# A list schedule replaced by written tables of the order, the engines and the buffer places

## The chip, the cores and the metric

The kernel runs on one core of a Trainium2 chip. The metric is device time in microseconds. The page of the profile calls the engines PE (TensorE, the matrix engine), PEld (its weight loads, which overlap), DVE (VectorE), ACT (ScalarE), POOL (GpSimd) and SP (SyncE). SP and POOL issue the DMA transfers here; each engine runs its instructions in the order in which the program issued them, and waits at each for what it needs.

## The reference

One layer of a hybrid backbone runs on 1024 latent tokens and 128 context tokens, all in float32. Cut to what matters:

```
h = rmsnorm(x, w) * (1 + scale1) + shift1          # scales, shifts, gates from silu(c) @ ada_w
u = h @ w_in                                       # 1024 -> 4288 columns
o_a = hgrn2_mixer(u[..., :P_A])                    # 4 heads x 128, forward and backward
o_b = rwkv7_mixer(u[..., P_A:])                    # 8 heads x 64, delta rule, both directions
x = x + gate1 * (concat([o_a, o_b]) @ w_out)
h = rmsnorm(x, w) * (1 + scale2) + shift2
gt = conv(h @ ffn_w_gate) + b                      # 3x3 on the latent grid, width 3 on the context
x = x + gate2 * ((gelu(gt) * (h @ ffn_w_up)) @ ffn_w_down)
y = rmsnorm(x, final_norm_w)
```

The outputs are both y and the final context states of the two mixers.

## The kernel before

The work is done in stages, but their instructions are mixed with one another. Line numbers are those of the profile of before.

- Start: nine row blocks of x are loaded (L1214), normed (L1148 to L1151, L1216), transposed on PE (L1208) and modulated into `hh` and `hl`, a high and a low part in the float32r format. `mod_columns` makes the modulation from `ada_w` (L1246, L1252).
- Projections: `proj` multiplies columns of `w_in` with the tokens, three float32r products for each (L1139 to L1141: high by high, low by high, high by low), 8 steps deep and 384 tokens wide. `load_w` fetches a column of weights on SP (seen as L1345 and L1306) and splits it.
- `features` prepares RWKV (small products L1474, L1475; copies of keys and values to DRAM at L1436, L1497 to L1503), `elim` solves its small systems, `chains` walks 18 chunks in each of two groups (L1790, L1804, L1837, L1844, L1852, L1861, L1863), `hgrn_block` and `hgrn_out` do HGRN (L1630 to L1753), `ada_block` the rest of the modulation (L1039, L1046, L1054). `wo_tile` is the output projection (L2033 to L2035, transposes at L2047).
- FFN: `product` (L2145) multiplies gate and up weights with quarter matrices, seven products in place of eight; `ffn_mid` does the convolution on DVE (L2234). `three` (L2310) is the down projection. The last row block is finished in two halves of 256 columns (L2432 to L2451), whose accumulators share one PSUM bank.

What decides the order: the kernel's text does not issue its instructions directly. Each call is recorded by `Plan` as an `Op`: one instruction, or a group that stays together. `close` finds what an op must wait for from the addresses that it reads and writes. An op may have several forms: `st` may issue a store on POOL or SP, `copy` may run on ACT or DVE. A tile belongs to a `Tag`, which has one or more places in a buffer.

`Plan.schedule` then runs a list scheduler over all 9618 ops. It estimates a cost for each op (`cost`, `pe_cost`, `wire`), takes the engine that is free first, ranks the ready ops by the length of the work behind them plus a lead (`LEADS`, and `NUDGE`, a number for every 16 ops of a kind), and takes off something for a change of the array's shape (`INTO`, `OUT`, `SWITCH`) or of an activation table. It chooses the form with the engine and the place that comes free first. `plan.ahead`, `plan.follow` and `plan.mark` give it hints. `Plan.issue` issues the ops in that order, engine by engine, and the framework adds the semaphores.

Of the kernel before, what the change touches and what calls it, by code (L numbers as in the profile page):

```python
# [20 lines left out]
P = 128  # L21
# [11 lines left out]
STRETCH = 2.76  # L33
LEAD_LAST = -10.47
LEAD_ADA = -9.0
LATE = 1.2
SWITCH = 2.0
FULL = 128, 128
INTO = 2.76
OUT = 0.86  # L40
HAM = 3.413
QUIET = 0.65
FETCH = 42.0
AHEAD = 240.0
HUNGRY = 2.04
BUSY = 168.59
ADDS = 2.1
NUDGE = {'step_kernel': [-1, 21, 23, 153, 19, -118, 24, 0, 59, 53, 38, -46, 7, -86, -57, -200, -162, -34, -65, 27, -37], 'const': [-1], 'turned': [45, 73, 123, 24, -81], 'param_loads': [-52, -27], 'params': [30, 141], 'first_columns': [-17, 0, 65, 95], 'mod_columns': [-200, 49, -70, -62], 'modulated': [34, -122, 14, -97, -13], 'conv_rkv': [-20, 28, 17, 14, -71, 21, 7, 6, 7, -131, -59, 65, -34, 2, -24, -4, -58, -28, -9, -11, -21, 2, -23, -64, -4, -36, -50, 143, 184], 'features': [6, -9, -1, 3, -13, 173, 166, 184, 184, 200, 149, -20, -36, 7, -27, -39, -22, -14, -14, -15, -12, -8, -18, -9, -17, 82, -12, 36, 109, 0, -7, 18, 92, -2, -53, -32, -50, 170, 95, 183, 157, 182, 192, 192, 196, 200, 169, 125, 124], 'hgrn_in': [-38, 41, -10, -9, -4, -40, -6, 65, 16, 167, 157, 136, 29, 21, 50, 30, -3, 3, 39, 5, 70, 11, 10, -19, -11, -16, -2, 19, -8, -14, -25, -37, -36, -37, -25, -62, -36, 154, -52, -90, -82, -96, -30, -38, -41, -30], 'elim': [17, 87, 0, -32, 20, -28, -25, -4, 80, -14, 86, 4, -1, -24, -14, 125, 199, 146, 179, 149, 76, 38, 74, 27, -3, -39, 69, 52, 13, -2, -7, 191, 129], 'chains': [-12, 7, 58, 70, 29, 57, 1, -9, -1, -10, 16, 18, 0, 0, 0, 4, 77, -53, 16, 8, 3, 30, -18, 35, 32, -33, 115, -29, 18, 40, 129, 1, -4, -10, 90, 82, 83, 76, 73, 184, 142, 17, 51, 4, 4, -8, -27, -45, 7], 'prep': [49, -75, 0, 82, 43, 31, 99, -43, 1, 33, -8, -70, 33, 4, -101, -13], 'bonus_rows': [49, -35, -103, -31, -186, -64], 'ada_block': [22, 5, -21, 0, 29, 23, 26, -1], 'hgrn_block': [31, -19, 139, -23, -94, -50, -93, -134, -96, 62, 82, 78, -23, 4, 4, -19, -18, -26, 49, 152, 4, 8, -95, -27, -41, -25, 87, 42, -65, 27, -3, 1, 1, -7, -23, 13, 61, 142, 176, 187, -16, 16, 9, 84, 186, 25, 34, 45, 8, 90, 104, 54, 12], 'hgrn_out': [8, -12, -31, -29, -73, -7, 20, 37, 0, 0, -66, 42, -18, 184, 5], 'mod_scale': [-188], 'wo_tile': [132, -14, -52, -13, -77, -45, 20, 14, 138, 89, 184, 105, 112, 117, 153, -46, 13, 104, 153, 65, -75, -18], 'post': [-28, -39, 124, -84, 61, 182, 99, 91, 98], 'stored': [164], 'put': [140, 90, 106, -49, -44], 'made': [131, -57], 'weights': [43, -44, 92, 147, 0, 8, -8, -18, 5, -12, -25], 'pair': [136, -34, 76, -16, 38, 4, 105, 37, -22, 7, -52, 10, 19, 14, -44, -32, -22, 5, -84, -73], 'product': [57, 177, 42, 46, 40, 20, 5, -5, 140, 121, 38, 192, -114, 25, 53, 97, 54, 40, 49, 185, 179, 184, 178, 64, 29, 32, 149, -6, 103, -18, -10, 4, -3, -2, 7, 12, -12, -55, -74, -88, 2, 2, -67, 65, 177, 23, 4, 22, 27, 36, 30, 41, 29, 17, 18, -12, 3, -18, -25, -52, -68, -48, -48, -31, 55, 41, 21, -34, -36, -36, -40, -56, -12, -27, -91, 8, -65], 'save': [105, 108, 53, 55, 13, 120, 47, 53, -164], 'front': [-17, -5, -19, 21, 73, 183, -1, -45, -50, 40, -69, 12, -29, -153], 'ffn_mid': [17, 31, -149, -11, 18, -24, 58, 51, 21, -13, 12, -149, -127, -154, -22, 26, -32, -74, -118, -29, -29, -24, -71, -200], 'down_sums': [-199, -96, 3, 17, -130, -141], 'rows_of_context': [-128, -42], 'tokens': [-35, -200, -165, -57, 82], 'part': [0, -36, -65, 9, 57, 17, -87, -74, -146, -145, -30, -154, -32, -28, -32, -63, -90, -146, 34, 112, -141, 13], 'weight': [0, 144, 90, 47], 'three': [-92, -24, -50, 1, 34, -59, -24, -5, -112, -198, -194, -193, -26, -159, -162, 89, -9, 200, 91, 195, -48, -47, -45], 'gate_row': [-16], 'kept': [-48], 'gated': [-101, -117, 49, 200, 19], 'normed': [-200, 181, -22], 'put_out': [-155, -71], 'total': [-200, -13, -29]}
LEADS = {'ada_block': 46.4, 'bonus_rows': 27.8, 'chains': -35.7, 'const': 113.0, 'conv_rkv': 0.0, 'down_weights': -36.2, 'elim': -4.6, 'features': 0.0, 'ffn_down': 14.5, 'ffn_mid': -1.7, 'finish': 52.5, 'finish_last': -12.3, 'first_columns': -38.6, 'front': 0.0, 'gate_row': 0.0, 'hgrn_block': -3.6, 'hgrn_in': 0.0, 'hgrn_out': 113.5, 'late': -0.7, 'made': 3.5, 'mod_columns': -1.2, 'mod_scale': 70.4, 'modulated': -24.2, 'pair': 8.2, 'param_loads': 9.6, 'params': -96.8, 'post': 3.0, 'prep': 119.5, 'product': -3.4, 'put': 0.0, 'save': 4.8, 'step_kernel': -1.0, 'stored': 0.0, 'three': -10.1, 'total': -0.3, 'turned': 4.0, 'weights': 0.0, 'wo_tile': 5.1}
# [88 lines left out]

class Op:
    __slots__ = ("id", "forms", "reads", "writes", "deps", "succ", "tiles", "tail", "start", "end", "left", "est",  # L140
                 "cost", "mode", "after", "kind", "wait", "place", "table", "dense", "lead", "area", "port", "wire", "dma", "words")
# [36 lines left out]
class Plan:  # L178


    PIECES = ("proj", "small_proj", "norm_rows", "modulate", "gate_rows", "load_step", "load_values", "conv_tiles")
    HELPERS = ("mm", "st", "copy", "combine", "split", "load_w", "record", "either", "acc", "fetch")
    ENGINES = ("PE", "DVE", "ACT", "POOL", "SP")
    BITS = 23
    ROW = 1 << 16
    LOW = (1 << 23) - 1
    TABLES = {"Ln": 1, "Sqrt": 2, "Gelu_apprx_tanh": 3, "Exp": 0, "Tanh": 0}
    last = None

    def __init__(self, tc, base):  # L190
        nc = tc.nc
        self.base = {F32: base, F32R: base.bitcast(F32R), I32: base.bitcast(I32)}
        self.tc = tc
        self.units = {"PE": nc.tensor, "DVE": nc.vector, "ACT": nc.scalar, "POOL": nc.gpsimd, "SP": nc.sync}
        self.ops, self.tags, self.tiles = [], {}, [None]
        self.live, self.group, self.chain_end, self.lead, self.boxes = {}, None, {}, 0.0, []
        self.first, self.mark, self.seen = None, 0, {}
        Plan.last = self
# [42 lines left out]
    def add(self, forms):  # L241
# [4 lines left out]
        line = f.f_lineno  # L246
        while f.f_code.co_name in self.PIECES:
            f = f.f_back
        self.kind = f.f_code.co_name
        forms = [(e, [(m, a, k, line)]) for e, m, a, k in forms]  # L250
        if self.group is not None:
            self.group.append(forms[0])
# [2230 lines left out]
```

## Time and profile before

| | |
|---|---|
| median of 3 runs | 1796.35 us (1785.7 to 1799.57) |
| profiled execution | 1795.13 us, its span 1793.4 us |
| PE busy | 1727.2 us, 96% of the span |
| DVE, ACT, POOL busy | 1459.4, 932.5 and 444.0 us |
| mean granted clock of PE | 0.992 |
| DMA | 352.99 MB moved, mean 197 GB/s |

The span is the time between the first and the last instruction that the profile shows. A matmul's duration in it overlaps with that of the next, so the distance between two starts tells what one costs. An idle time is shown in square brackets with what ended it; "issue" means that nothing in the profile did.

### The profile page before, as it was taken

The page shows a single profiled execution, that of the slowest core. Times are in us where ns is not written, and L with a number is a line of the kernel's source. Part 1 is how long each engine was busy: PE and PEld are TensorE (multiplying, and loading weights), DVE is VectorE, ACT ScalarE, POOL GpSimd, SP SyncE. Part 2 cuts the span into 40 slices and gives each one's busy share as a digit, 9 for nine tenths or more (in the row PEclk, how much of TensorE's full clock was granted, in tenths as well). Part 3 has the DMA queues.
Part 4 walks back from the last instruction along what each step waited for, and adds up shares of the span by engine and source line. Part 5 has one row for each costly group of instructions (what it writes and reads, how often), then busy time and mean ns, then how long its engine had stood idle before and what let it go on. Part 6 is the DMA issues. An engine that isn't in the chain of part 4 may idle for free. (4 is left out here: it accounts for less than half of the span.)

```text
span 1793.4 us, 44872 instructions
## 1 busy us (share of the span) xinstructions
PE 1727.2 (96%) x17726; PEld 1548.7 (86%) x17726; DVE 1459.4 (81%) x2799; ACT 932.5 (52%) x1907; POOL 444.0 (25%) x708
## 2 busy tenths in 40 slices
PE   6999999999999989999999999999999999999998
PEld 4898888889988878887777889999999999888886
DVE  6559988987788868887777877998988889979875
ACT  6556757552266545663545754444444444665542
POOL 2003334263323222233211122233233333100000
PEclk9999999999999999999999999999999999999999
DMA  9326447497676578898987657678787778997674
GB/s 321 100 63 175 109 123 172 109 228 202 187 220 196 178 222 265 265 308 249 312 240 250 226 129 147 133 172 174 153 165 162 156 139 173 288 327 221 212 254 146
DMA packets 320148, 352.99 MB, mean 197 GB/s; under 512 B 66420, under 2 KB 238242, under 8 KB 319585
## 3 DMA queue, kind: packets, MB, share of 16 engines
q1 hardware_dynamic: 253520, 245.18, 45.7%
q0 software_dynamic: 66416, 104.95, 25.2%
q8 instruction: 139, 2.28, 0.5%
q14 instruction: 73, 0.59, 0.1%
HBM read 254.99 MB, written 118.10 MB: 208 GB/s over the span
## 5 line engine op out<-in xcount | busy, mean ns | idle before, releaser
L1139 PE MATMUL banks<-hh,wh 128*128 128x384 f32 x768 | 279.7, 364 | 1.4 <-DVE fx L1327 1.4
L1141 PE MATMUL banks<-hh,wl 128*128 128x384 f32 x768 | 258.4, 336 | 0.0
L1140 PE MATMUL banks<-hl,wh 128*128 128x384 f32 x768 | 258.1, 336 | 0.0
L2234 DVE SCALAR_TENSOR_TENSOR low<-low,pf 128x1024 f32<-128x1024 f32 x176 | 225.2, 1281 | 12.2 <-ACT low L2228 9.7
L2145 PE MATMUL banks<-qm,wh 128*128 128x320 f32 x968 | 223.5, 310 | 1.6 <-DVE low L2204 1.3
L2145 PE MATMUL banks<-hbm,wh 128*128 128x256 f32 x880 | 165.0, 284 | 1.5 <-DVE low L2013 1.5
L2145 PE MATMUL banks<-qm,wl 128*128 128x320 f32 x528 | 163.1, 309 | 0.2 <-DVE wl L2115 0.2
L2145 PEld LDWEIGHTS banks<-qm,wh 128*128 128x128 f32 x968 | 160.8, 189 | 2.1 <-DVE low L2204 1.5
L1139 PEld LDWEIGHTS banks<-hh,wh 128*128 128x128 f32 x768 | 144.9, 189 | 19.6 <-issue 10.9
L1140 PEld LDWEIGHTS banks<-hl,wh 128*128 128x128 f32 x768 | 145.2, 189 | 2.0 <-issue 1.2
L1141 PEld LDWEIGHTS banks<-hh,wl 128*128 128x128 f32 x768 | 144.6, 188 | 0.0
L2145 PEld LDWEIGHTS banks<-hbm,wh 128*128 128x128 f32 x880 | 140.3, 191 | 2.3 <-DVE low L2013 1.8
L2145 PE MATMUL banks<-ham,wh 128*128 128x256 f32 (+1 forms) x616 | 132.7, 295 | 0.0
L2145 PE MATMUL banks<-hbm,wl 128*128 128x256 f32 x440 | 124.8, 284 | 0.0
L2183 ACT COPY fx<-banks 128x320 f32<-128x320 f32 (+1 forms) x132 | 52.4, 398 | 111.6 <-PE banks L2145 111.6
L2145 PEld LDWEIGHTS banks<-ham,wh 128*128 128x128 f32 x616 | 102.1, 191 | 0.1
L2145 PEld LDWEIGHTS banks<-qm,wl 128*128 128x128 f32 x528 | 99.1, 188 | 0.8 <-DVE wl L2115 0.8
L2115 ACT CAST wh<-low 128x512 fp32r<-128x512 f32 x88 | 54.4, 619 | 65.8 <-DMA low<-in_ffn_w_up_dram 42.5
L2145 PEld LDWEIGHTS banks<-hbm,wl 128*128 128x128 f32 x440 | 84.4, 192 | 0.0
L2145 PE MATMUL banks<-ham,wl 128*128 128x256 f32 (+1 forms) x264 | 77.3, 293 | 0.0
L2115 DVE TENSOR_TENSOR wl<-low,wh 128x512 fp32r<-128x512 f32 x88 | 60.3, 687 | 9.9 <-ACT wh L2115 9.5
L2115 ACT CAST wh<-wr 128x512 fp32r<-128x512 f32 x66 | 39.8, 621 | 47.8 <-PE banks L2145 27.6
(595 smaller groups left out, 4444.1 us busy)
## 6 DMA issues: line engine op xcount, KB each, us to landing
wr<-in_w_in_dram SPq DMA_DIRECT2D x34, 512.0 KB, 5.5
d_t<-in_ffn_w_down_dram POOLq DMA_DIRECT2D x55, 256.0 KB, 6.3
low<-d_a SPq DMA_DIRECT2D x51, 256.0 KB, 5.3
low<-d_ak SPq DMA_DIRECT2D x64, 192.0 KB, 5.7
low<-in_ffn_w_gate_dram SPq DMA_DIRECT2D x44, 256.0 KB, 3.2
low<-in_ffn_w_up_dram POOLq DMA_DIRECT2D x44, 256.0 KB, 5.0
d_a<-low POOLq DMA_DIRECT2D x19, 576.0 KB, 4.0
low<-d_kb SPq DMA_DIRECT2D x36, 256.0 KB, 5.8
```

Source lines behind the costliest of these rows:

```text
L1139: mm(o, wh[:, kt, :], hh[:, kt, c], kt == 0, False)
L1140: mm(o, wh[:, kt, :], hl[:, kt, c], False, False)
L1141: mm(o, wl[:, kt, :], hh[:, kt, c], False, kt == KT - 1)
L2115: split(*w, src)
L2145: pe.matmul(o, a[:, kt, :], b[:, kt, :], start=start and first, stop=last, skip_group_check=not start)
L2183: act.copy(keep[n], y[:, 0:w])
L2234: dve.scalar_tensor_tensor(av, shifted(dy, dx), tap(3 * dy + dx), av, MUL, ADD)
```

## The change

`schedule` no longer plans. Three tables take the place of its decisions: `SEQUENCE`, the numbers of all ops in the order in which they are issued; `ENGINE_OF`, a letter for each of the 1500 ops that have more than one form; `PLACE_OF`, a digit for each tile whose tag has more than one place. They were found by a local search on the sequence itself. The costs, leads, nudges and hints go. The recorded work and the finding of dependences stay, and the assertions make sure that the order keeps the dependences and that no two live tiles share a place.

```
-STRETCH = 2.76
-LEAD_LAST = -10.47
...
-NUDGE = {...}
-LEADS = {...}
+SEQUENCE = [int(i) for i in """
+1 2 17 6 18 19 0 12 13 14 15 7 11 177 184 10 27 28 4 3 20 21 29 30 33 22 24 16 34 26 31 32
...
+""".split()]
+ENGINE_OF = (
+    "VVVAVAVAAAAAAVAVVVAVAAAVGGGGGSGGGGGSSGSSGGGAVAVVVAAVVVVAVVAVAAAAVVAVVVAAVVVVVAVAGASASASASASVSASVVAGAASVAVASGSSAAAASSGSAAASAASAAAASSSSVAVASGSSAA
...
+PLACE_OF = (
...
     def schedule(self):
-        ops = self.ops
-        for op in ops:
-            for d in op.deps:
-                ops[d].succ.append(op.id)
...
+        by = iter(ENGINE_OF)
+        for op in self.ops:
+            if len(op.forms) > 1:
+                e = self.LETTER[next(by)]
+                op.forms = [f for f in op.forms if f[0] == e]
+        spot = iter(PLACE_OF)
+        for rec in self.tiles[1:]:
+            t = rec[0]
+            rec[2] = t.places[int(next(spot), 36) if len(t.places) > 1 else 0]
+        self.order = [self.ops[i] for i in SEQUENCE]
...
-    with plan.ahead(900.0):
-        ld(cr[0], I["c"].rearrange("l (a b) -> (l a) b", b=128))
...
+    ld(cr[0], I["c"].rearrange("l (a b) -> (l a) b", b=128))
...
-                plan.follow("dense")
```

Compared op by op, half of the 9618 ops stand within 24 places of where they stood and one in a hundred over 162 away. Of the 1500 with a choice, 242 go from POOL to SP and 71 from SP to POOL, 138 from DVE to ACT and 61 from ACT to DVE, 23 from ACT to POOL and 14 back. Of the 2526 tiles with a choice 1547 lie elsewhere. SP issues 1185 DMAs (1014 before), POOL 357 (528), DVE has 2724 instructions (2801) and ACT 1942 (1872).

The changed file is shorter, so its lines have other numbers: L1139 to L1141 are now L1070 to L1072, L1659 is L1582, L1748 is L1671, L1804 is L1727, L1844 is L1767, L1852 is L1775, L2310 is L2229; L1345, L1306, L1436, L1497, L1500 and L1502 are L1268, L1229, L1359, L1420, L1423 and L1425.

The first place is on PE, in the mixed stage, where `chains` and `hgrn_block` run beside the fourth `ada_block`. `hh`, `hl`, `wh` and `wl` are a projection (full array), `low` to `low` with 64x64 a step of a chain (shape 128*64), `top` with 32x32 a step of HGRN (128*32), and `c_ident` a transpose (full array). Before:

```order
L1852 MATMUL banks<-low 64x64 x8
L1139 MATMUL banks<-hh,wh_133 128x384
L1140 MATMUL banks<-hl,wh_133 128x384
L1141 MATMUL banks<-hh,wl_135 128x384
L1804 MATMUL banks<-c_ident,low 128x128 x4
L1659 MATMUL banks<-top 32x32 x12
L1748 MATMUL banks<-c_ident,top 128x128 x3
L1844 MATMUL banks<-low 64x64 x8
L1659 MATMUL banks<-top 32x32 x12
L1139 MATMUL banks<-hh,wh_133 128x384
L1140 MATMUL banks<-hl,wh_133 128x384
L1141 MATMUL banks<-hh,wl_135 128x384
```

The same instructions in the change:

```order
L1775 MATMUL banks<-low 64x64 x8
L1582 MATMUL banks<-top 32x32 x12
L1727 MATMUL banks<-c_ident,low 128x128 x4
L1070 MATMUL banks<-hh,wh_134 128x384
L1071 MATMUL banks<-hl,wh_134 128x384
L1072 MATMUL banks<-hh,wl_135 128x384
L1671 MATMUL banks<-c_ident,top 128x128 x3
L1070 MATMUL banks<-hh,wh_134 128x384
L1071 MATMUL banks<-hl,wh_134 128x384
L1072 MATMUL banks<-hh,wl_135 128x384
L1767 MATMUL banks<-low 64x64 x8
L1582 MATMUL banks<-top 32x32 x12
```

The four groups on the full array stand together now, so the array's shape changes four times along these rows instead of six. Over the whole of PE's order it changes 445 times instead of 543.

The second place is the end of PE's order, the two halves of the last row block (`qm`, `ham`, `hbm`, `wh`, `wl` hold weights and activations there; three rows of one kind are one step). Semaphore waits are shown in brackets. Before:

```order
L2310 MATMUL banks<-qm,hbm 128x256 x3
L2310 MATMUL banks<-ham 128x256 [waits DVE_49]
L2310 MATMUL banks<-ham 128x256 x2
L2310 MATMUL banks<-qm,ham 128x256 [waits DVE_49]
L2310 MATMUL banks<-qm,ham 128x256 x2
L2310 MATMUL banks<-qm,hbm 128x256 x3
L2310 MATMUL banks<-qm 128x256 [waits Activation_49]
L2310 MATMUL banks<-qm 128x256 x2
L2310 MATMUL banks<-ham,qm 128x256 x3
```

In the change:

```order
L2229 MATMUL banks<-hbm,ham 128x256 x3
L2229 MATMUL banks<-ham,qm 128x256 [waits DVE_49]
L2229 MATMUL banks<-ham,qm 128x256 x2
L2229 MATMUL banks<-qm,wl_136 128x256 x3
L2229 MATMUL banks<-hbm,qm 128x256 x3
L2229 MATMUL banks<-qm,hbm 128x256 x3
L2229 MATMUL banks<-ham,hbm 128x256 x3
L2229 MATMUL banks<-wh_134,qm 128x256 x3
L2229 MATMUL banks<-qm,hbm 128x256 [waits Activation_49]
L2229 MATMUL banks<-qm,hbm 128x256 x2
```

One wait for DVE is gone, and six steps run between the two waits that are left; two more steps of the second half now stand behind the first half.

The third place is SP, early in `features`, between the fetch of a weight column for HGRN (`wr`, L1306) and the next one for RWKV (L1345); `d_kb`, `d_ak` and `d_v` are DRAM buffers that are stored to. Before:

```order
L1306 DMA wr<-in_w_in_dram 128x8x128
L1502 DMA d_kb_82<-top 64x6x64
L1500 DMA d_kb_82<-top 64x6x128
L1502 DMA d_kb_82<-top 64x6x64
L1500 DMA d_kb_82<-top 64x6x128
L1497 DMA d_ak_78<-top 128x6x128
L1345 DMA wr<-in_w_in_dram 128x8x128
```

In the change:

```order
L1229 DMA wr<-in_w_in_dram 128x8x128
L1425 DMA d_kb_82<-top 64x6x64
L1420 DMA d_ak_78<-top 128x6x128
L1423 DMA d_kb_82<-top 64x6x128
L1425 DMA d_kb_82<-top 64x6x64
L1359 DMA d_v_84<-top 128x3x128 x2
L1420 DMA d_ak_78<-top 128x6x128
L1425 DMA d_kb_82<-top 64x6x64 x2
L1268 DMA wr<-in_w_in_dram 128x8x128
```

Nine stores stand between the two fetches where there were five.

524 lines of the change are left out of this document (84 added, 440 removed), and 300 rows, old and new, of the table SEQUENCE.

## The prediction

> **What bounds the kernel now.** I read the page first, then the busy times by stage, then who PE waits for, then single stretches of the timeline.
>
> ```profile
> span 1793.4 us, 44872 instructions
> PE 1727.2 (96%) x17726; PEld 1548.7 (86%) x17726; DVE 1459.4 (81%) x2799; ACT 932.5 (52%) x1907; POOL 444.0 (25%) x708
> ```
>
> TensorE (PE) is busy for 96% of the span, so everything below is about PE: what time it idles, and what time it is "busy" without being useful. The next answer cuts the span into the start, the mixed stage (projections, RWKV and HGRN work), the dense stage (both halves of the FFN) and the tail. The first number after the window is its length, the next PE's busy time, then weight loads, VectorE, ScalarE and GpSimd; the last three are the granted clock, the DMA share and GB/s.
>
> ```profile
> core 0: us, PE busy (x) PEld busy (x) DVE busy (x) ACT busy (x) POOL busy (x), PEclk, DMA share, GB/s
> 0.00:36.00 36.00, 20.84 (x159) 14.48 (x159) 22.36 (x61) 23.94 (x50) 11.74 (x34) 1.00 0.96 315
> 36.00:1056.00 1020.00, 979.07 (x12869) 852.85 (x12867) 823.26 (x1813) 562.23 (x1202) 279.11 (x510) 0.99 0.68 200
> 1056.00:1781.00 725.00, 723.67 (x4687) 678.62 (x4686) 609.85 (x916) 344.25 (x650) 153.16 (x164) 1.00 0.76 189
> 1781.00:1793.40 12.40, 3.63 (x19) 2.72 (x17) 3.96 (x11) 2.03 (x6) 0.00 (x0) 0.65 0.20 75
> ```
>
> Idle time of PE is length less busy: 15.2 us in the start, 40.9 in the mixed stage, 1.3 in the dense stage, 8.8 in the tail. The dense stage cannot get faster by a new order: it has the same matmuls and nothing to fill. The start has its DMA engines 96% busy with bytes that the change does not alter. So the mixed stage is where an order can matter. PE's waits, longest in total first (us in total, times, longest):
>
> ```profile
> PE banks L1208 <- DVE top L1216: 6.3, 2, 5.2
> PE banks L1852 <- issue: 5.2, 2, 4.0
> PE banks L1208 <- DVE low L1149: 5.1, 1, 5.1
> PE banks L1474 <- DVE top L1465: 3.9, 3, 3.1
> PE banks L1790 <- DMA low<-d_ak: 3.0, 5, 1.3
> PE banks L1474 <- DVE top L1466: 2.4, 2, 1.2
> ...
> PE banks L1659 <- DVE top L1688: 1.1, 1, 1.1
> ```
>
> The two L1208 rows belong to the start. The others are many short waits, most of them for VectorE, at different lines. Only one is long: 4.0 us put down to nothing ("issue"), so no order of the work is shown to be its cause.
>
> **The change part by part.** No instruction is added or removed: 9618 records before and after, the same matmuls, the same transfers. What moves is the order, the engine of 1500 records that may go to either of two, and the place of tiles in their buffers. Half of the records stand within 24 places of where they stood, so this is a reshuffle nearby and not another plan.
>
> *Array shapes.* Every small matmul uses a part of the array, and the third column of the trace's rows says which (128*32, 128*64, 64*128 and so on). Here is what a change of shape costs, in the rows of one stretch (start, duration, then the line):
>
> ```profile
> 540.64 0.40 PE L1665 MATMUL banks<-top 128*32 128x32 f32 x24
> 540.97 0.44 PE L1139 MATMUL banks<-hh,wh 128*128 128x384 f32 x1
> 541.25 0.34 PE L1140 MATMUL banks<-hl,wh 128*128 128x384 f32 x1
> 541.42 0.34 PE L1141 MATMUL banks<-hh,wl 128*128 128x384 f32 x1
> 541.60 0.34 PE L1139 MATMUL banks<-hh,wh 128*128 128x384 f32 x1
> ...
> 542.47 0.34 PE L1141 MATMUL banks<-hh,wl 128*128 128x384 f32 x1
> 542.73 0.57 PE L1671 MATMUL banks<-top 128*64 128x64 f32 x12
> ```
>
> From one dense matmul to the next, 541.25 to 541.42, it takes 0.17 us. The first one after the shape 128*32 takes 0.28 (540.97 to 541.25), and leaving for 128*64 takes 0.26 (542.47 to 542.73). So entering costs 0.11 and leaving 0.09 us, 0.10 on the mean. Counted along PE's printed order, the shape changes 543 times before and 445 times in the changed kernel, 98 fewer, nearly all in the mixed stage. PE is busy for 96% of that stage, so little of this hides: 98 x 0.10 x 0.96 = 9.4 us off. Bounds: 5 if half of the saved changes lay under waits, 14 if the unseen pairs of shapes cost 0.15.
>
> *Waits in the mixed stage, 40.9 us.* The order decides them, and so does the load of VectorE, which the rows above name most. Of the records with a choice, 138 move from VectorE to ScalarE and 61 the other way, 77 net. A row of this kind is
>
> ```profile
> L1846 DVE COPY low<-banks 64x256 f32<-64x256 f32 x19 | 7.9, 421 | 9.2 <-ACT low L1846 5.0 <-PE banks L1844 3.9
> ```
>
> 0.42 us, so 77 x 0.42 = 32 us leave VectorE. It is busy for 823 of 1020 us there; 791 would leave it 229 us free where it has 197, a sixth more. If waits fell only as free time rises they would fall by a sixth, 7 us. If the new order removed all but the 4.0 us of "issue" they would fall by 37. I take a third, 14 us, nearer to the first because that is the end that a row shows. The other bound is a rise: the waits are short and spread, and moving neighbours past each other makes new ones as easily; up to half as much again, +20.
>
> *The clock.* PE's clock dips to half for some microseconds in places of the mixed stage and at its end:
>
> ```profile
> 300.00:350.00 50.00, 47.21 (x423) 42.52 (x418) 46.73 (x103) 27.27 (x55) 16.68 (x30) 0.97 0.52 135
> ...
> 600.00:650.00 50.00, 45.45 (x849) 38.93 (x848) 38.51 (x91) 28.59 (x68) 12.74 (x23) 0.93 0.67 212
> ...
> 850.00:900.00 50.00, 46.77 (x719) 40.27 (x720) 40.45 (x93) 28.58 (x58) 13.15 (x22) 0.97 1.01 321
> ...
> 1000.00:1050.00 50.00, 45.06 (x229) 37.53 (x228) 39.72 (x76) 38.29 (x87) 9.48 (x12) 0.97 0.71 216
> 1050.00:1100.00 50.00, 50.00 (x366) 49.98 (x366) 42.58 (x62) 25.93 (x51) 10.05 (x9) 0.96 0.51 107
> ```
>
> The shortfalls of the clock, 0.03 + 0.07 + 0.03 + 0.03 + 0.04, times 50 us make 10 us, and the windows up to 1050 have 2.8 to 4.9 us of idle PE in them. If idle time falls by a third I let this fall by a third as well: 3 us. Bounds 0 and 8.
>
> The Trainium skill, "TensorE: Matmul & The Clock Gate", Part 1, says that the clock halves after an idle window of about 3.4 us. By that rule only the 4.0 us wait could have caused a dip, and the change would win nothing on this term, which would make the sum 3 us smaller. The trace speaks against so narrow a reading: the other four windows dip without that wait, and past the start the longest other one in PE's list is 3.1 us.
>
> *Start and dense stage.* Zero each. The start is covered by DMA (96% busy); if that cover were gone, the 15.2 us of idle PE would be at stake, but only a smaller load would do that. Bounds 3 us either way.
>
> *The tail.* Row block 7 is finished in two halves of 256 columns that share a PSUM bank, with the last matmuls stopped by the work on the first half:
>
> ```profile
> 1780.87 0.52 PE L2310 MATMUL banks<-qm,hbm 128*128 128x256 f32 x3
> 1781.43 0.43 DVE L2439 TENSOR_TENSOR banks<-banks,fx 128x256 f32<-128x256 f32 x1 [1.68 <-PE banks L2310]
> 1781.91 0.42 PEld L2310 LDWEIGHTS banks<-ham 128*128 128x128 f32 x3 [0.73 <-DVE banks L2439]
> ...
> 1783.05 0.41 PEld L2310 LDWEIGHTS banks<-qm,ham 128*128 128x128 f32 x3 [0.72 <-DVE low L2440]
> ...
> 1784.67 0.71 PEld L2310 LDWEIGHTS banks<-qm 128*128 128x128 f32 x3 [0.85 <-ACT banks L2441]
> 1785.27 0.76 PEld L2310 LDWEIGHTS banks<-ham,qm 128*128 128x128 f32 x3
> ```
>
> Three waits of 0.7 to 0.85 us, with one, two and two groups of three matmuls behind them. In the changed order there are two waits, and six groups run behind the first one in a row. One stop of about 0.7 us goes, and some of the half-speed end: 1 us off. Bounds 0 and 2.
>
> *Sum:* 9.4 + 14 + 3 + 1 = 27.4 us. The profiled execution took 1795.13 us (span 1793.4 and 1.7 around it), so 1767.7; the median of the three runs shown is 1796.35, 1.2 above it. I say 1768.
>
> **The rivals.** *Only the shapes count:* the waits are not removed but change places, since each record that moves ahead of another makes that one later, and the clock dips with them. Then 9.4 + 1 go: 1784.7. For it speaks that the waits are short and at many lines, with no common cause; against it that VectorE really has less to do.
>
> *The waits nearly vanish:* all but the "issue" wait and the dips: 9.4 + 37 + 8 + 1 = 55 off, 1740. For it: PE has ready work in most places, as its dense projections can be put anywhere. Against it: VectorE at 81% in the stage cannot always be ahead.
>
> *SyncE's queue becomes late, and the kernel slower.* SP carries all loads. Of the stores that may go to either queue 242 move from POOL to SP and 71 back, so SP issues 1185 transfers instead of 1014. It takes them in order: a store whose data is not there holds up every load behind it. Rows of today (the first two for PE and SP, the last for what a store waits on POOL):
>
> ```profile
> PE banks L1790 <- DMA low<-d_ak: 3.0, 5, 1.3
> ...
> SPq L1345 <- DVE wl L1345: 38.6, 5, 12.7
> ...
> POOL d_hf L1325 <- ACT fx L1323: 38.3, 15, 11.3
> ```
>
> A store waits 38.3 / 15 = 2.6 us on POOL. If 171 more of them wait so on SP, that is 440 us of its queue. SP is today the one that waits for buffers (38.6 us at the weights' tile alone), so most of it is cover; if one microsecond in ten reached PE, 44 us would be lost against the 10 won: 1829. It turns slower at one in 40. Against it: the loads that make PE wait cost only 3.0 us now, and SP's place in the order was chosen with its stores.
>
> The Trainium skill, "DMA: Bandwidth & Descriptors", section "Issuing engines are not separate DMA queues", says that using several issuing engines saves only sequencer time, since the same 16 DMA engines do the work. By that rule the moved stores land no sooner from SP, and only its sequencer's time is at stake, as in this rival.
>
> **How the numbers follow.** Forecast, 1768: 50%, its own range 1756 to 1779. Only the shapes, 1784.7: 25%. Waits nearly vanish, 1740: 13%. SP's queue, above 1797: 12%. About 1% is what measurements of this kernel can tell, so the limits stand at 1778.4 and 1814.3. Faster by more than 1%: 47 of the first 50 and the 13, 60%. Slower by more than 1%: most of the last case, 9%. Within 1%: 31%. The range is 1743 to 1797: it holds the forecast and the first rival, and half of the second. The bounds of the terms (5 to 14, 37 to -20, 8 to 0, 2 to 0) reach from 1734 to 1810; the ends past the range are left to the two outer cases.
>
> **What would show it.** PE's idle time between 36 and 1056 us should be near 27 us instead of 40.9, and the dense stage should keep its 725 us, beginning about 27 us sooner. Between equal neighbours the 0.11 and 0.09 us should stand as before, only less often. VectorE's busy time should be about 32 us lower and ScalarE's higher. PE's clock in the mixed stage should lose fewer than 10 us. The tail from the last whole row block should be 1 us shorter. The forecast is wrong if PE idles for 40 us or more in the mixed stage, if loads (d_ak, w_in, d_kb) show up as what PE waits for, or if the dense stage grows.

## The result and the profile after

The changed kernel takes 1775.55 us in the median of 6 runs (1770.57 to 1779.31), the kernel before 1797.49 in 6 runs. The ratio is 0.9885, with a 95% interval of 0.9855 to 0.9916: faster by 1.15%, 21.9 us. The forecast was 1768, range 1743 to 1797.

The profiled execution of the changed kernel took 1778.03 us, 17.1 less than that of before. Its page begins:

```profile
span 1776.3 us, 44618 instructions
PE 1711.1 (96%) x17726; PEld 1544.9 (87%) x17726; DVE 1424.9 (80%) x2722; ACT 949.4 (53%) x1977; POOL 354.6 (20%) x546
```

VectorE has 34.5 us less to do, ScalarE 16.9 more and GpSimd 89.4 less, as the moved records said. But PE's idle time, span less busy, was 1793.4 - 1727.2 = 66.2 us and is 65.2. The whole gain stands in PE's *busy* time, 16.1 us lower with the same 17726 matmuls. The same stages as in the prediction (length, PE busy, then the other engines, clock, DMA share, GB/s):

```profile
0.00:36.00 36.00, 22.77 (x151) 15.47 (x154) 20.55 (x60) 23.38 (x49) 9.52 (x29) 0.86 0.91 299
36.00:1041.00 1005.00, 961.53 (x12874) 847.97 (x12867) 788.88 (x1732) 583.38 (x1269) 198.39 (x365) 0.99 0.70 203
1041.00:1766.00 725.00, 724.02 (x4691) 679.17 (x4690) 611.95 (x923) 340.63 (x655) 146.72 (x152) 1.00 0.76 189
1766.00:1776.30 10.30, 2.74 (x21) 2.34 (x20) 3.49 (x10) 2.03 (x6) 0.00 (x0) 0.87 0.20 76
```

The mixed stage took 1020 us and takes 1005. (The bounds of after are set 15 us earlier, so that the 725 us of the dense stage are a choice; the matmul of that stage that stood at 1056 us stands at 1042.) PE's idle time in it is 1005 - 961.53 = 43.5 us, where it was 40.9 and 27 was forecast. What PE waits for now, longest in total first (us, times, longest):

```profile
PE banks L1713 <- DMA low<-d_ak: 5.8, 4, 2.5
PE banks L947 <- DVE top L945: 4.1, 1, 4.1
PE banks L1767 <- ACT low L1762: 3.2, 3, 1.6
PE banks L1138 <- DVE low L1145: 2.9, 1, 2.9
PE banks L1775 <- DVE top L1611: 2.5, 1, 2.5
PE banks L1582 <- DVE top L1583: 2.3, 4, 0.9
```

L947 and L1138 belong to the start. The others are again short and at many lines, but few are those of before: the 4.0 us of "issue" are gone, 2.5 us at L1775 and 2.5 us at the load of d_ak have come. The waits were exchanged, not removed.

To see what became of PE's time I split it by the distance between the starts of successive matmuls. A distance longer than the median of the same instruction between its equals has an excess. Idle time is taken out; the rest goes to "change" where the shape differs from the matmul before, else to "slow", which holds the half-clock stretches too, with the changes of shape that fall in them. Base and parts add up to the span. In us:

| | before | after | difference |
|---|---|---|---|
| at the median pace, with the ends | 1539.3 | 1539.6 | 0.3 |
| idle within the stream of matmuls | 55.5 | 54.2 | -1.3 |
| at changes of shape at full clock (556 and 446) | 75.0 | 61.2 | -13.8 |
| slow at an unchanged shape or at half clock | 123.6 | 121.3 | -2.3 |
| span | 1793.4 | 1776.3 | -17.1 |

The third row overstates what the changes won, since it leaves out those in half-clock stretches, 6 before and 17 after, with about 1 and 4.5 us. With them the changes are 562 and 463, and they cost 10 us less as they stand, or 12 less if those at half clock are put at the 0.137 us of the others: 0.10 to 0.12 us for each change saved, and about two thirds of the gain of this execution. The fourth row hides two opposite parts: at an unchanged shape and full clock the matmuls cost 6 to 10 us less, by the choice of the median, spread over many lines, and at half clock about 5 us more.

The rows at the changes read as before (start, duration; an entry from the shape 128*64, then a transpose on the full array):

```profile
588.12 0.57 PE L1594 MATMUL banks<-top 128*64 128x64 f32 x12
588.62 0.44 PE L1070 MATMUL banks<-hh,wh 128*128 128x384 f32 x1
588.90 0.34 PE L1071 MATMUL banks<-hl,wh 128*128 128x384 f32 x1
589.08 0.34 PE L1072 MATMUL banks<-hh,wl 128*128 128x384 f32 x1
...
590.82 0.49 PE L1622 MATMUL banks<-c_ident,top 128*128 128x128 f32 x3
591.06 0.42 PE L1070 MATMUL banks<-hh,wh 128*128 128x384 f32 x1
591.32 0.34 PE L1071 MATMUL banks<-hl,wh 128*128 128x384 f32 x1
591.50 0.34 PE L1072 MATMUL banks<-hh,wl 128*128 128x384 f32 x1
```

The first dense matmul takes 588.62 to 588.90, 0.28 us, where the next take 0.17 to 0.18: 0.11 for the entry, as in the prediction. After the transpose, whose shape is the same, it takes 0.26 too. That row became a question for the experiments.

### The profile page after: what moved, and what is told of

It reads as the page before. It is cut to its first block, busy times and chain, and to the rows that moved or that the text cites. A ratio compares the mean times of both kernels' runs of the same rounds, so it can differ in the third digit from the quotient of the medians.

```text
span 1776.3 us, 44618 instructions
## 1 busy us (share of the span) xinstructions
PE 1711.1 (96%) x17726; PEld 1544.9 (87%) x17726; DVE 1424.9 (80%) x2722; ACT 949.4 (53%) x1977; POOL 354.6 (20%) x546
## 4 chain that ended last, share of the span: by engine, by line
PE 73%; DVE 4%; DMA 4%; ACT 3%; issue 1%; POOL 1%; SPq 0%; DVEq 0%; ACTq 0%; POOLq 0%
PE banks L2065 27%; PE banks L2229 14%; PE banks L1070 4%; PE banks L1072 4%; PE banks L1071 4%; PE banks L1713 2%; PE banks L1955 1%; PE banks L1957 1%; PE banks L1956 1%; PE banks L1582 1%; PE banks L1784 1%; PE banks L1627 1%; PE banks L1760 1%; PE banks L1767 1%; PE banks L1786 1%
## 5 line engine op out<-in xcount | busy, mean ns | idle before, releaser
L1070 PE MATMUL banks<-hh,wh 128*128 128x384 f32 x768 | 278.2, 362 | 0.6 <-DVE fx L1250 0.6
L1072 PE MATMUL banks<-hh,wl 128*128 128x384 f32 x768 | 258.7, 337 | 0.0
L2153 DVE SCALAR_TENSOR_TENSOR low<-low,pf 128x1024 f32<-128x1024 f32 x176 | 225.7, 1282 | 10.6 <-ACT low L2147 8.0
L1070 PEld LDWEIGHTS banks<-hh,wh 128*128 128x128 f32 x768 | 144.8, 188 | 15.7 <-issue 9.3
L1072 PEld LDWEIGHTS banks<-hh,wl 128*128 128x128 f32 x768 | 144.9, 189 | 0.0
L2102 ACT COPY fx<-banks 128x256 f32<-128x256 f32 (+1 forms) x132 | 52.0, 397 | 110.2 <-PE banks L2065 98.2
L2035 ACT CAST wh<-low 128x512 fp32r<-128x512 f32 x82 | 50.5, 618 | 69.4 <-PE banks L2065 60.5
L2035 DVE TENSOR_TENSOR wl<-low,wh 128x512 fp32r<-128x512 f32 x82 | 56.2, 689 | 22.8 <-ACT wh L2035 20.7
L2035 ACT CAST wh<-wr 128x512 fp32r<-128x512 f32 x72 | 44.6, 622 | 54.3 <-PE banks L2065 43.8
```

The source lines that it names most:

```text
L1070: mm(o, wh[:, kt, :], hh[:, kt, c], kt == 0, False)
L1072: mm(o, wl[:, kt, :], hh[:, kt, c], False, kt == KT - 1)
L2035: split(*w, src)
L2102: act.copy(keep[n], y[:, 0:w])
L2153: dve.scalar_tensor_tensor(av, shifted(dy, dx), tap(3 * dy + dx), av, MUL, ADD)
```

## The experiments

Times are medians; each run's ratio to the kernel before carries its 95% interval. "After" is the changed kernel, 1775.55 (0.9855 to 0.9916). The runs were made at different times and on different chips; the medians of the kernel before beside them, where it ran several times, lie between 1795.9 and 1798.7 us, so a difference of two medians is good to about 3 us. The parts in the text are those of the table above, for the run's own profiled execution.

**1. More changes of shape, nothing else.** One of 51 moves:

```diff
 L1299 MATMUL banks<-low,fx 128x384
+L1070 MATMUL banks<-hh,wh_133 128x384
+L1071 MATMUL banks<-hl,wh_133 128x384
+L1072 MATMUL banks<-hh,wl_136 128x384
 L1462 MATMUL banks<-top 32x32 x16
-L1070 MATMUL banks<-hh,wh_133 128x384
-L1071 MATMUL banks<-hl,wh_133 128x384
-L1072 MATMUL banks<-hh,wl_136 128x384
```

> The changed kernel, with 51 dense groups on PE (one high-low product of a projection each, about 0.5 us) taken out of their runs and put between two small steps that stood side by side, within 6 us of their place: the array's shape changes 67 times more, nothing else is moved. Shapes theory: a change costs 0.10 us (the two rows of the prediction) to 0.137 us (75.0 us of excess at 556 changes in the trace of before), so 67 x 0.10 to 0.137 = 7 to 9 us slower than the changed kernel's 1775.5, near 1783, and the excess at changes of shape in the trace rises from 61.2 by that much. Rival, the gain came from waits: the excess rises but the waits give it back, or the 0.5 us that a small step comes later counts in full, 51 x 0.5 = 25 us, near 1800.

Measured 1784.36 us, ratio 0.9933 (0.9908 to 0.9958): 8.8 us slower than after. At the changes 61.2 became 70.7 us, but that is not the price of 67 changes alone: 4 changes of this run fall in half-clock stretches, where 17 of after do. With them the changes cost 5.6 us more as they stand and 7.7 more at the price of the others, 0.08 to 0.12 for each of the 67. Idle rose by 3.6. The price is there and reaches the end; the 25 us of the rival did not come.

**2. Fewer changes of shape in the kernel before.** One of 55 swaps:

```diff
-L1070 MATMUL banks<-hh,wh_133 128x384
-L1071 MATMUL banks<-hl,wh_133 128x384
-L1072 MATMUL banks<-hh,wl_135 128x384
 L1299 MATMUL banks<-low,fx 128x384
+L1070 MATMUL banks<-hh,wh_133 128x384
+L1071 MATMUL banks<-hl,wh_133 128x384
+L1072 MATMUL banks<-hh,wl_135 128x384
```

> The kernel before, with 55 pairs of neighbouring groups on PE swapped where that joins groups of one shape: 69 changes of shape fewer, the order of all other engines, the engines and the places of before kept. Shapes theory: 69 x 0.10 to 0.137 = 7 to 9.5 us off 1797, near 1789. Rival, grouping alone is worth nothing because a step that goes later makes new waits: 1797 or above, with PE's idle time higher by 5 to 10 us. Rival, the gain is the engines and the queue: 1797.

Measured 1797.92 us, ratio 1.0011 (0.9985 to 1.0036): nothing won. The trace says why: the changes fell by 8.4 us (75.0 to 66.6), 0.12 each, and idle rose by 6.0 (55.5 to 61.5). The second theory was right: moved for the sake of a group, steps make new waits. Fewer changes alone do not make the gain; they are won only *without more waits*.

**3, 4. The engines and the queue of before, under the new order.** Only letters of `ENGINE_OF` differ, here in ScalarE's order for the first and in SyncE's for the second:

```diff
+L1150 COPY top<-banks 128x384 x3
...
-L1150 COPY top<-banks 128x384 x7
-L1150 COPY fx<-banks 128x384
...
-L1020 DMA top<-in_ffn_conv_dram 110x128
 L1172 DMA low<-in_ada_w_dram 128x2x256 x2
```

> The changed kernel's order and places, but the 236 records that went from one of VectorE, ScalarE and GpSimd to another (138 from VectorE to ScalarE among them) go back to the engine of before. PE's order stays. Prediction's theory, relief of VectorE removes waits: VectorE gets 32 us of work back and PE's waits in the mixed stage come back by up to 14 us, near 1790. Rival, only the shapes count: within 4 us of 1775.5. Third, the engines were chosen together with the order, so that any other choice is worse whatever its load: more than 14 us slower, with the waits for VectorE and ScalarE both up.

Measured 1825.03 us, ratio 1.0171 (1.0136 to 1.0206): 49.5 us slower than after and 27.6 slower than before, the third theory. Idle is 84.4 us (54.2), the changes stand at 61.9. The clock has a part in it: its mean is 0.986 over the six executions, 0.994 in those of after, which by the span makes about 14 of the 49.5 us (an estimate). The new order with the old engines is worse than either kernel.

> The changed kernel's order and places, but the 313 stores that went from one of GpSimd and SyncE to the other go back (242 to GpSimd, 71 to SyncE), so SyncE issues 1014 transfers as before. Rival of the prediction, a late SyncE queue is paid for in the changed kernel: the wait for d_ak (5.8 us) and part of the others go, 4 to 10 us faster than 1775.5. Shapes theory: the queue is cover, within 4 us. Third, GpSimd's work is on a path now: slower by over 5 us, with waits for GpSimd or for DMAs in PE's list.

Measured 1784.35 us, ratio 0.9947 (0.9924 to 0.9970): 8.8 us slower. Moving stores to SyncE *won* time, so the rival that feared SyncE's queue had the wrong queue. The trace of this run shows one place. GpSimd's queue there, and VectorE behind it (start, duration, in brackets the idle time and its releaser):

```profile
380.29 0.95 POOL L1475 MEMSET fx<- 32x1024 f32 x1
381.29 0.84 POOL L1683 MEMSET low<- 64x768 f32 x1
...
384.56 0.85 POOL L1420 DMA_DIRECT2D d_ak<-top  x1
```

```profile
385.94 0.56 DVE L1417 TENSOR_TENSOR top<-low,top 128x384 f32<-128x384 f32 x1
389.29 0.56 DVE L1388 TENSOR_TENSOR top<-top 128x384 f32<-128x384 f32 x1 [2.79 <-DMA d_ak<-top]
```

The store in the third row is one that went back to GpSimd. It takes 0.85 us of that engine and lands 4.6 us after its issue. VectorE's L1388 needs the place in `top` that the store reads, and waits 2.79 us for it. PE then waits 2.8 us for VectorE at L1397, its longest wait in this stretch, and its clock is halved from 391.1 for 6.8 us. Over the whole run idle rose by 8.3 us.

**5. Waits filled.** 22 groups that were ready are put ahead of a step at which PE waited. One of them:

```diff
+L1353 MATMUL banks<-c_ident,low 128x128 x3
+L1070 MATMUL banks<-hh,wh_134 128x384
+L1071 MATMUL banks<-hl,wh_134 128x384
+L1072 MATMUL banks<-hh,wl_135 128x384
 L1343 MATMUL banks<-hsum,top 128x2 x3
-L1353 MATMUL banks<-c_ident,low 128x128 x3
-L1070 MATMUL banks<-hh,wh_134 128x384
-L1071 MATMUL banks<-hl,wh_134 128x384
-L1072 MATMUL banks<-hh,wl_135 128x384
```

> The changed kernel, with 22 groups on PE put ahead of a step at which PE waited 0.4 us or more in its profiled execution (dense groups that were ready then, from within 8 us behind it; 13.4 us of work by their durations there, in 34.8 us of such waits). 4 changes of shape more, nothing else is moved. Theory that a wait on PE is a hole that other work can fill: 13.4 less 4 x 0.137 and what the filled step comes later, 6 to 13 us off 1775.5, so 1763 to 1770. Rival, waits only change places, because the next step waits for the same chain of VectorE and ScalarE work: within 3 us of 1775.5, with PE idle as long as in the changed kernel (54 us inside its stream) at other lines.

Measured 1773.64 us, ratio 0.9878 (0.9860 to 0.9896), 1.9 us under after, which these intervals do not separate from nothing. Its waits in the mixed stage:

```profile
PE banks L1713 <- DMA low<-d_ak: 3.7, 4, 1.5
PE banks L977 <- DMA top<-in_ada_w_dram: 3.5, 1, 3.5
PE banks L1767 <- ACT low L1762: 3.3, 3, 1.8
PE banks L1582 <- issue: 2.6, 3, 1.5
PE banks L1775 <- issue: 2.3, 1, 2.3
```

The 2.5 us at d_ak went, and 3.5 us for a load of `ada_w` came, which cost nothing like that before. 13.4 us of work were put into waits, idle fell by 5.1 and the changes and the slow part gave 3.6 of it back. So most of the wait that was filled came again further on. The rival was right about the time, but not that idle would stay as it was; that it is the same chain of VectorE and ScalarE steps which makes PE wait, as it says, was not tried.

**6, 7. VectorE's load, both ways.** The exchange between VectorE and ScalarE undone by halves, again in `ENGINE_OF` alone (ScalarE's order, first run, then second):

```diff
-L1179 COPY low<-banks 128x256
-L1150 COPY fx<-banks 128x384
...
+L1150 COPY top<-banks 128x384 x3
```

> The changed kernel, but the 138 records that went from VectorE to ScalarE go back to VectorE; the 61 that went the other way stay. VectorE has 138 x 0.42 = 58 us more work. Load theory (of the prediction): PE's waits grow with VectorE's load, so this half of the exchange is the harmful one, slower than the whole exchange undone (1825). Rival, order and engines fit each other: each record that is not where the order has it costs about the same, 50 us / 236 = 0.21 us, so 138 of them cost about 29 us, near 1804, and the waits for VectorE and for ScalarE both grow.

> The changed kernel, but the 61 records that went from ScalarE to VectorE go back to ScalarE; the 138 stay there. VectorE has 61 x 0.42 = 26 us less work than in the changed kernel, ScalarE more (it is busy for 53% only). Load theory (of the prediction): faster than 1775.5, by up to a third of 26 us, or at least not slower. Rival, order and engines fit each other: 61 x 0.21 = 13 us slower, near 1788, although VectorE has less to do.

Measured 1810.54 us, ratio 1.0082 (1.0064 to 1.0101), and 1779.29 us, ratio 0.9916 (0.9893 to 0.9938): 35.0 and 3.7 us slower than after, the 3.7 not separated from nothing by the intervals. Their busy times, in this order:

```profile
PE 1716.8 (95%) x17726; PEld 1544.7 (86%) x17726; DVE 1474.7 (82%) x2860; ACT 896.0 (50%) x1839; POOL 352.2 (20%) x546
```

```profile
PE 1708.0 (96%) x17726; PEld 1541.1 (87%) x17726; DVE 1404.3 (79%) x2661; ACT 969.8 (55%) x2038; POOL 349.8 (20%) x546
```

Neither theory holds alone. With 50 us more of VectorE's work the kernel is 35 us slower, and with 20 us less it is still not faster. If each record costs m for being off its place in the order and v for its load on VectorE, then 138 (m + v) = 35.0 and 61 (m - v) = 3.7, so m = 0.16 and v = 0.10 us. That is an estimate from two equations, not shown by itself. By it the 77 net records of the change are worth 7 us, half of the forecast's 14, and between 2 and 10 if the 3.7 is anything from 0 to 12. Run 3, with 236 records and 77 net, would cost 45 us by it, and cost 49.5.

**8, 9. The price of a change by itself.** In the dense stage PE waits for nothing, so small matmuls can be added there and only their price is seen:

```diff
+                    if e == "PE" and line == self.PRODUCT and k["start"]:
+                        begun += 1
+                        o, x, y = [fix(z) for z in a]
+                        for _ in range(1):
+                            self.at(line)(partial(self.units[e].matmul, o[0:32, 0:64], x[:, 0:32], y[:, 0:64],
+                                                  start=True, stop=True))
```

The second run has `range(11 if begun % 11 == 1 else 0)` there.

> The changed kernel with 132 small matmuls added in the dense stage, one ahead of each accumulation of the FFN's gate and up products (128x32 of the stationary operand, 64 columns, into the region that the accumulation then overwrites, so nothing of the result changes). Each stands alone between dense ones: 264 changes of shape more. PE has no waits there, so all of it is on the path. At 0.10 us a change: 26 us and the matmuls' own time (0.03 to 0.06 us each, 4 to 8 us), 1806 to 1810; at 0.137 us: 36 and 4 to 8, 1816 to 1820; if a change costs nothing there: 1780 to 1784.

> The same 132 small matmuls as in the run beside it, but eleven together at every eleventh accumulation: 24 changes of shape more instead of 264. At 0.10 us a change: 2.4 us and 4 to 8 us of their own, 1782 to 1786, that is 24 us less than the spread ones; at 0.137: 33 us less than those; if a change costs nothing: the same as those.

Measured 1785.57 us, ratio 0.9943 (0.9921 to 0.9965), and 1777.20 us, ratio 0.9891 (0.9860 to 0.9923): 8.4 us apart for 240 changes, 0.035 each. Both prices of the expectation failed, by factors of three and four. The added matmuls were float32r, though, and the small steps of the kernel are plain float32.

**10, 12. Shape or format.** The same with float32, then five kinds in turn:

```diff
+                        for n, dt in self.KINDS[begun % 5]:
+                            self.at(line)(partial(self.units[e].matmul, o[0:n, 0:64], x[:, 0:n].bitcast(dt),
+                                                  y[:, 0:64].bitcast(dt), start=True, stop=True))
...
+    KINDS = [[(128, F32)], [(32, F32)], [(64, F32R)], [(128, F32R)], [(64, F32), (32, F32)]]
```

> As the spread probe, but the added small matmuls are in plain float32, the format of the small steps in the mixed stage (128x64 of the stationary operand, 64 columns): one ahead of each of 132 accumulations, five ahead of every third. The reading is the time from group to group in the trace, with none, one and five of them ahead. In float32r a pair of changes took 0.08 us there. If the price of a change is the array's, it is 0.08 again and the rest of each group grows by the matmul's own time only; if it belongs to the format, the pair takes about 0.2 us, the sum of the two prices in the prediction.

> Five kinds of small additions in turn, one ahead of each of 132 accumulations of the dense stage (float32r, full array), each with 64 columns moving and overwritten afterwards: float32 on the full array (only the format differs), float32 on 128x32 (format and shape), float32r on 128x64 (only the shape), float32r on the full array (nothing differs), and float32 128x64 followed by float32 128x32 (format, and a change of shape among the small ones). Read from the trace: the time from the dense matmul before to the third one after, less three dense ones and less the addition's own passes (0.03 us for each of float32r, two of 0.058 us in float32). Shape theory of the prediction: 0.2 us for the second, third and fifth kind (0.3 in the fifth), nothing for the first and fourth. Format theory, after the two probes (0.08 us a pair in float32r, 0.34 us in float32): about 0.25 to 0.34 for the first, second and fifth, 0.08 for the third, nothing for the fourth.

Rows of the run with five kinds. A group of the accumulation has three matmuls; the addition is shown merged with the first two of its group ("x3" is one float32r addition and two dense matmuls, "x4" one of float32, for which the trace has two passes):

```profile
1295.98 0.31 PE L2074 MATMUL banks<-qm,wl 128*128 128x320 f32 x1
1296.13 0.62 PE L2074 MATMUL banks<-ham,wh 128*128 128x64 f32 x4
1296.59 0.28 PE L2074 MATMUL banks<-ham,wl 128*128 128x256 f32 x1
...
1307.12 0.31 PE L2074 MATMUL banks<-qm,wl 128*128 128x320 f32 x1
1307.35 0.79 PE L2074 MATMUL banks<-qm,wh 128*32 128x64 f32 x4
1307.98 0.31 PE L2074 MATMUL banks<-qm,wl 128*128 128x320 f32 x1
```

From the dense matmul before to the third after: 1295.98 to 1296.59 is 0.61 us with the addition on the full array, and 0.147 + 0.120 + 0.120 of it are the usual distances of dense matmuls with 320 and 256 columns, which leaves 0.22. 1307.12 to 1307.98 is 0.86 with the one on 128x32, less three times 0.147 leaves 0.42. The medians over all places:

| added | time added, us | own passes | left |
|---|---|---|---|
| float32r, full array (nothing differs) | 0.109 | 0.03 | 0.08 |
| float32r, 128x64 (shape) | 0.108 | 0.03 | 0.08 |
| float32, full array (format) | 0.222 | 0.116 | 0.11 |
| float32, 128x32 (format and shape) | 0.422 | 0.116 | 0.31 |
| float32, 128x64 (run 10) | 0.450 | 0.116 | 0.33 |
| float32, 128x64 and then 128x32 | 0.684 | 0.232 | 0.45 |

The own passes are the distances inside the runs of eleven and of five, 0.032 and two of 0.058 (measured for 128x64 and taken for all of float32). A narrow shape costs nothing in float32r: 0.108 against 0.109. In float32 it costs 0.422 - 0.222 = 0.20 for the two changes of a visit, and 0.684 - 0.450 - 0.116 = 0.12 for one among narrow float32 steps. So neither theory had it: the price needs both, the shape and the format. The probe of run 8 is explained as well: 120 visits more than in run 9, at 0.08, make 9.6 us, where 8.4 were measured. The Trainium skill, "TensorEngine Tiling (Array Packing)", section "Key Properties", says that changing the tiling mode drains the TensorE; the narrow float32 rows agree, the float32r rows show no cost of that kind.

Where a visit of float32 128x32 pays its 0.31 us shows in the distances: 0.09 more from the dense matmul to the first narrow pass, 0.02 between the narrow passes, 0.09 from the last one to the dense matmul, and 0.11 from this one to the next dense one. The last piece is 0.08 in every visit, also where nothing differs.

With these prices the orders can be counted out. Between dense and narrow steps the kernel goes 268 times before and 198 times after; to a transpose or another full float32 step 167 and 205 times; from such a step to a narrow one 173 and 129; among narrow ones 121 and 136. At 0.31 and 0.11 for two changes of the first two kinds and 0.10 and 0.12 for one of the others (0.10 is taken from the pair, not measured there) this makes 82 and 71 us, 11 less. Of these 9.6 stand at the changes of shape themselves, where a visit pays 0.20 of its 0.31 us; the trace has 10 to 12 there.

**11. Other places.** A third of the change that no other run touches: digits of `PLACE_OF`.

```diff
-    "310276100824813248516210123021231201310310312130214301010010100123401234110601210324110037602011430004157401203104253100101010101001010110101021010101"
+    "310276100824813243556710123031231201310300312331214301010010100123401234011607110324101023602011430117145401203104253100101010101001010110101021010101"
```

> The changed kernel's order and engines; 311 of the 2526 tiles with a choice go to the free place whose last user lies furthest back in the sequence, instead of the place in the table. Theory that the third table matters little (waits for a free place are not what PE's list shows): within 4 us of 1775.5. Rival, the places in the table were chosen with the order: over 5 us slower. Rival, waits for places are hidden behind the engines' names and an older place removes some: over 4 us faster.

Measured 1782.38 us, ratio 0.9913 (0.9887 to 0.9939): 6.8 us slower than after (5.0 by the ratios, whose intervals overlap), with 6.0 us more idle. The second theory, by a small margin. A place that has been free for longer was not better here. The places of before were not put back, so this run does not say what the change of places won.

## Why the prediction was right and where it failed

The forecast of 1768 us (its own sum, with the 1.2 us added, is 1768.9) was 7.5 below the median, and the direction and the range were right. But the sum got there with a wrong term, and two of its own signs of being wrong came: PE idles for 43.5 us in the mixed stage, where 40 was the limit, and d_ak heads the list of what PE waits for. That the time came out so near is in part luck: the 14 us of waits did not come, and 6 to 10 us at matmuls of unchanged shape came, which the sum does not have.

*Array shapes, 9.4 us.* Right: 10 to 12 us at the changes in the trace, 9.6 there by the prices of runs 8 to 12, inside the bounds of 5 to 14. The two prices read from one stretch, 0.09 and 0.11, are two of the four pieces of a visit in run 12, within 0.01 us; the 0.09 on the way back was overlooked, and most of the 0.11 belongs to any visit and not to the shape. These two errors nearly cancel. What the step did not see either is that saved changes are not yet saved time: in run 2 they were paid back in waits.

*Waits in the mixed stage, 14 us.* This step failed. PE's idle time there was to fall to 27 us and rose to 43.5. The argument was that VectorE's free time grows by a sixth, so waits fall by a sixth to a third. VectorE did get 34.5 us off, and runs 6 and 7 say that this is worth something, 2 to 10 us by the estimate. But the waits do not simply follow VectorE's load: with 20 us less of it, run 7 had none fewer. And in run 5 most of the wait that was filled came again elsewhere. That it comes from chains of steps between PE, VectorE and ScalarE is argued from the rows of PE's list (L1767 for ScalarE's L1762, L1775 for VectorE's), not shown. What the engines, the queue and the places of the tables do is to let the changes of shape fall without the waits rising: the engines and the queue of before put back cost 49.5 and 8.8 us, other places for 311 tiles 6.8, with 30.2, 8.3 and 6.0 us more idle time of PE. The rival "only the shapes count", at 1784.7, had this mechanism and about the right size for it; what it lacked is the matmuls of unchanged shape and the clock.

*The clock, 3 us.* About right in size, but not for its reason. The two profiled executions show nothing won: PE ran at half clock for 31.2 us before and for 35.4 us after, of which 20.5 lie in the mixed stage in both. But one execution says little here. Those of the other kernels had between 13.5 us (run 7) and 46.1 us (run 3), and the profiled one of after has the lowest granted clock of its six, 0.991. Over all executions on record with their clock its mean is 0.9907 for the kernel before (59, on four chips) and 0.9937 for the changed one (6). What is missing to full clock, times the span, is 16.6 and 11.2 us, 5.4 us less. That is an estimate of what the clock won, and a high one where a dip fell into a wait; the bounds were 0 and 8. The reason given, a third less idle time, did not come in the profiled execution, so why the clock is higher is not shown.

*Start 0, dense stage 0, tail 1.* The start stayed as it was: the operation at 36.0 us stands at 36.7 now, with 10.2 us of half clock ahead of it in this execution, where before had none. The dense stage won 4 us in its first 100 us (its first product begins 10.6 us earlier, the same matmul at 1150 stands 14.7 earlier), where a half-clock stretch of 6.8 us at 1047 is gone, and 1.3 us between 1500 and 1536; that is past the bound of 3. At 1700 the same matmul is 16.0 us earlier and the span ends 17.1 us earlier, so about 1.1 us come from the tail. The rows there:

```profile
1764.24 0.52 PE L2229 MATMUL banks<-hbm,ham 128*128 128x256 f32 x3
1764.80 0.43 DVE L2357 TENSOR_TENSOR banks<-banks,fx 128x256 f32<-128x256 f32 x1 [1.26 <-PE banks L2229]
...
1765.74 0.42 PEld L2229 LDWEIGHTS banks<-ham,qm 128*128 128x128 f32 x3 [1.19 <-DVE low L2358]
...
1768.77 0.42 PEld L2229 LDWEIGHTS banks<-qm,hbm 128*128 128x128 f32 x3 [0.85 <-ACT banks L2359]
```

Two waits instead of three, as read from the order.

*SyncE's queue.* Given 12% and refuted by run 4: the loads of d_ak do show up with 5.8 us where they had 3.0, but the stores cost more on GpSimd. (SP does not carry all loads, as this rival says: GpSimd issues loads of FFN weights, 3 of them in the mixed stage.)

The profiled executions differ by 17.1 us and the medians by 21.9. The 5.4 us of clock, of which the profiled pair shows nothing, would fill that gap, by the estimate above. What stays open is why matmuls of unchanged shape cost 6 to 10 us less at full clock: the prices of runs 8 to 12 give 1.7 us of it, less time after the return from a visit, and no run shows the rest.

## What to carry to other kernels

Before counting a wait of the busiest engine at its length, fill it and see whether it comes back: 13.4 us of work put into waits won 1.9 us here. Order, engines and places that were found together have a price only together: engines or queue changed alone cost 9 to 50 us here, and a lighter load on VectorE won nothing. The clock differs between executions of one kernel (0.991 to 0.996 in the six of after) by as much as was to be won with it; take it from all executions, not from the profiled one. Read the price of a change of shape separately for each format, and count it over a whole visit, since a third of it lies between two dense matmuls after the return.

## What the runs showed of the hardware

The half-clock stretches begin on a grid of 3.41 us. Of 72 such stretches in fourteen profiled executions 61 came right behind one of 3.41 us in which PE was busy for 60% or less. Three of the changed kernel, each with the stretch ahead of it (length, PE busy, and the clock as the third figure from the end):

```profile
285.40:288.80 3.40, 3.31 (x104) 2.46 (x94) 2.08 (x2) 3.40 (x6) 0.00 (x0) 1.00 0.93 212
288.80:292.20 3.40, 3.40 (x49) 2.96 (x52) 3.04 (x6) 2.12 (x5) 0.91 (x2) 0.50 0.60 159
623.30:626.70 3.40, 1.13 (x21) 1.20 (x22) 1.41 (x6) 1.19 (x4) 1.10 (x2) 1.00 0.75 222
626.70:630.10 3.40, 3.40 (x71) 3.01 (x71) 1.54 (x5) 1.25 (x3) 0.00 (x0) 0.50 0.40 133
906.60:910.00 3.40, 1.06 (x16) 1.09 (x16) 2.87 (x8) 1.29 (x3) 1.44 (x2) 1.00 0.78 257
910.00:920.20 10.20, 9.67 (x156) 7.77 (x154) 2.73 (x10) 2.47 (x7) 0.97 (x2) 0.50 0.74 238
```

The waits of 2.5 us that ended at 626 and at 909 were each followed by one, so a wait can cost more than itself. The first is another matter: PE was busy for 3.31 of 3.40 us, but with work like this (line, form and count, then busy us and mean ns):

```profile
L1462 PE MATMUL banks<-top 32*32 32x32 f32 x52 | 2.1, 227 | 0.0
L1464 PE MATMUL banks<-top,fx 32*32 32x32 f32 x32 | 1.1, 227 | 0.1
...
L1464 PE MATMUL banks<-top 32*32 32x32 f32 x22 | 0.9, 228 | 0.0
```

106 of its 112 matmuls from 285.3 on are 32x32, on a sixteenth of the array. Six of the fourteen executions have a dip at this place, and these are all that came behind a window with PE busy for over 90%; that the small matmuls are the reason is argued, not tried. The Trainium skill, "TensorE: Matmul & The Clock Gate", Part 1, gives a free-running window of 3413 ns and a clock that halves after an idle window. The grid and the half agree; the window need not be idle.

Counted the other way, from the windows of the grid at full clock, from 36 us on and without the last 20 us of each execution: all 21 with PE busy below 40% were followed by a half-clock one, 7 of 9 between 40 and 50%, 11 of 52 between 50 and 60%, and 11 of about 7000 above. PE's busy time is not all of it: in run 1 a stretch at 631 with PE busy for 46% (1.55 of 3.40 us) had no dip behind it.
